# A decoder block in fp32 halves: narrower pooling columns, a second seven-product group in w_o, and another order at the front of the MLP

## The chip, the cores and the metric

One core of a Trainium2 chip. The time is device microseconds of one execution of the whole program; the figure for a kernel is the median of its timed runs. Beside the timed runs one execution is recorded by the hardware profiler, and the views below come from that one.

## The reference

One layer: a combined projection of the normed input, causal pooling over four windows, a gated depthwise convolution, two sigmoid gates, the projection w_o, and an MLP with squared relu. Sequence 256 behind 16 meta tokens, model width 2048, MLP width 8192, all fp32.

```python
u = rms_norm(h, g_pre_mix)                     # h: 16 meta rows and 256 tokens
z_pool, v_conv, g_conv, gate_a, gate_b = split(u @ w_in)
# pooling group g (256 columns of z): mean over the last 2, 4, 8 or 16 tokens, minus the token
y_a = causal_multiscale_pool(z_pool, w_pool_grp, pool_scale) @ w_pool_out
y_b = conformer_conv(v_conv, g_conv, w_dw, b_dw, ln_g, ln_b) @ w_conv_out
m = sigmoid(gate_a) * y_a + sigmoid(gate_b) * y_b
h = h + rms_norm(m @ w_o, g_post_mix)
u = rms_norm(h, g_pre_mlp)
f = square(relu(u @ w_up)) @ w_down
h = h + rms_norm(f, g_post_mlp)
return h[:, 16:]
```

## The kernel before

**Products in halves.** An fp32 weight block of 128 x 2048 elements (1 MB, tile `raw`) is loaded by a DMA on SP's queue, cast on ACT to a rounded `hi` (1.91 us), and subtracted on DVE to the rest `lo` (2.29 us). The activations exist as such a pair too. A product of the two is three terms, hi times both halves and lo times the high half; where 256 tokens stand in both halves of one 512-column operand, that is 8 matmuls with hi and 4 with lo for a 512-deep block, 12 with 512 columns.

**Stages, in the order of the trace.** Start and transposes of x (to 35 us), the projections for v and g (to 107), the projection for z (`project(..., mm=mm3, width=L)`, four calls, one for each pooling group, 96 matmuls of L = 272 columns each; to 154.6), the gates (to 329) with the pooling and the depthwise convolution on DVE beside them, the grouped pooling map `acc_grp`, the two output projections po and co (to 424.9), w_o (to 510.6), the residual and the transposes for the second norm (to about 547), and the MLP in pieces (to 1189).

**z and the pooling.** `evac_z` multiplies a PSUM tile of z by the row factor `rb` on DVE. `pool_items` sums windows by doubling: level g adds the previous level to itself, shifted by 2^g columns. A window of 2, 4, 8 or 16 tokens needs 2, 4, 8 or 16 columns at most ahead of the 256 tokens; all four groups have 16.

**w_o.** The weight is 4 x 4 blocks of 512 x 512, block (kb, n) being rows kb and columns n. STEPS lists the work in PE's order. `Xnk` (column block n, rows k) is a plain step: two products, one for each half of the tokens, into the banks c0n and c1n. P1 to P7 are the seven products of a fast 2 x 2 scheme on rows 0 and 1 and columns 0 and 1: each takes a sum of blocks of w_o (`add_rooms` on DVE, 2.29 us, or `add_second`, a DMA on POOL's queue that accumulates a block onto one that is there) and a sum of parts of m (`forms_o`, four of them), and goes to bank a, b or a c bank. `GIVES_O` says to which c banks a product is given further: ACT copies the bank to a part of `og`, DVE adds or subtracts it. Banks a and b take the place of the tiles `mt` in which the last part of m was transposed (PE at line 898, ACT's cast m<-mt at 902, DVE's subtraction m<-mt at 905). There are 31 products: seven P and two for each of twelve X. The residual's input h1 (2 MB) is loaded on POOL's queue ahead of the co projection (L944). The w_o blocks go through three to five rooms `raw`.

**The order.** The class `Plan` collects work items: an engine, a cost in us, what they read and write, and a lateness. PE and SP keep the order in which items were added. For the other engines due times are worked out backwards from PE's, and a simulation with the costs picks what starts next; `emit` then writes the instructions. So a cost or a lateness changes no instruction but can change the order on ACT, DVE and POOL. One plan covers w_o, another the MLP.

**The front of the MLP.** Up to L1831 the plan holds the end of the first up product (banks `acc_up`), eight squares of h1 on ACT (`square_h1`, L987 in the trace) for the second norm, their sum (`mean2`, L1540), the root, `diag2` (rsqrt at L446 to L450, the power of two p2 and its diagonal at L1550 to L1553, and five small operations for eps2 at L1554 to L1559), and the first MLP loads. `up_done` empties a bank: ACT copies half of it (half<-..., L1578), DVE adds the other half to it (F_raw<-half,..., L1585). The second up product goes into two banks `bank_u` (L496 with hi, L502 with lo). The splits of the blocks raw_a, raw_c and raw_m are casts at L1496 and subtractions at L1500.

Of the kernel before, what the change touches and what calls it, by code (L numbers as in the profile page):

```python
# [115 lines left out]
def hybrid_block(ctx: ExitStack, tc: tile.TileContext, ins: dict, out: bass.AP):  # L116
# [559 lines left out]

    def evac_z(j0):
        def f(j, acc):
            nc.vector.tensor_mul(z[:, j0 + j, :], acc[:, :L], rb)
# [12 lines left out]
    def pool_items(g):  # L692
# [7 lines left out]
        def add(q):  # L700
            def f():
                nc.vector.tensor_add(dst[:, q:q + GK, lo_:], src[:, q:q + GK, lo_:],
                                     src[:, q:q + GK, lo_ - w:L - w])
            return f
# [181 lines left out]

    pairs_room = big.tile([P, 3, 2 * T], F32, tag="ux", name="pairs")
# [55 lines left out]
    h1 = big.tile([P, NT, D], F32, tag="k8", bufs=2, name="h1")  # L943
    nc.gpsimd.dma_start(h1, xv)  # L944
# [52 lines left out]
    def m_of(k):  # L997
# [7 lines left out]
    B_OF = {"P1": (0, 0), "P2": (1, 0), "P3": (1, 1), "P5": (0, 0), "P6": (0, 0), "P4": (0, 0),  # L1005
            "P7": (1, 1)}
    A_OF = {"P1": (0, 0), "P2": (0, 1), "P4": (1, 1)}
    FORM_OF = {"P3": SA4, "P5": SA1, "P6": SA2, "P7": SA3}
    INTO = {"P1": "a", "P2": "c00", "P3": "c01", "P5": "b", "P6": "a", "P4": "c10", "P7": "a"}
# [13 lines left out]
    room_at = {(1, 0): 0, (2, 0): 1}  # L1023
    steps = STEPS.split()

    def raw_key(s):

        return B_OF[s] if s[0] == "P" else (int(s[2]), int(s[1]))

    def source_o(key):  # L1030
        return columns(w_o, key[0] * CK, CK, key[1] * CW)[0][0]
# [5 lines left out]
    for i, s in enumerate(steps):  # L1037
        key = raw_key(s)
        last_use[key] = i
        if s == "P4":  # L1040
            last_use[B_OF["P2"]] = i
        if key not in wanted and key not in room_at:
            wanted.append(key)
# [20 lines left out]
    def add_second(room):  # L1064

        src = source_o((0, 1))
# [10 lines left out]
    def split_room(i, room, rows=CK, up=False):  # L1077
# [13 lines left out]
        plan.add("ACT", 1.91, high, reads=(f"raw{room}",), writes=(f"hi{q}",))  # L1091
        plan.add("DVE", 2.29, low, reads=(f"raw{room}", f"hi{q}"), writes=(f"lo{q}",))

    def add_rooms(to, room):
        a_, b_ = room_of[to][:, :CK * CW], room_of[room][:, :CK * CW]
        plan.add("DVE", 2.29, lambda: nc.vector.tensor_add(a_, a_, b_),
                 reads=(f"raw{to}", f"raw{room}"), writes=(f"raw{to}",))

    def weights_o(i):
        s = steps[i]  # L1100
        room = room_at[raw_key(s)]
        if s == "P6":
            add_rooms(room, room_at[B_OF["P3"]])
            add_second(room_at[B_OF["P3"]])
        if s == "P4":
            add_rooms(room, room_at[B_OF["P2"]])
        if i >= 2:
            split_room(i, room)
        if s == "P1":
            add_second(room)  # L1110
        for key, last in last_use.items():
            if last == i:
                free_rooms.append(room_at[key])
        loads_o()

    def forms_o(f):
        dst, src, name = Sf[:, f[0], f[1]], A[:, f[0], f[1]], f"S{f[0]}{f[1]}"
        plan.add("ACT", 0.68, lambda: nc.scalar.copy(dst[:, :, 0, :], src), reads=("A",),
                 writes=(name,))
        plan.add("DVE", 0.70, lambda: nc.vector.tensor_sub(dst[:, :, 1, :], src,  # L1120
# [13 lines left out]
    begun = set()  # L1134

    def product_o(i):
# [15 lines left out]
        bank = INTO[s]  # L1152
        if s in A_OF:
            form, names = m_block(*A_OF[s]), []
        else:
            at_ = FORM_OF[s]
            form, names = (lambda k, a_: Sf[:, at_[0], at_[1], k, a_, :]), [f"S{at_[0]}{at_[1]}"]
        add(bank, form, names, s in ("P1", "P5") or bank not in begun, True)
        if s in GIVES_O:
            j = "ab".index(bank)  # L1160
            st = og[:, j, block(NB - 1)]
            plan.add("ACT", 0.62, lambda: nc.scalar.copy(st, banks_o[bank]), reads=(bank,),
                     writes=(f"st{j}",))
            for t, n, sign in GIVES_O[s]:
                def f(name=f"c{t}{n}", add_=(nc.vector.tensor_add if sign > 0 else
                                             nc.vector.tensor_sub)):
                    add_(banks_o[name], banks_o[name], st)
                plan.add("DVE", 0.69, f, reads=(f"st{j}",), writes=(f"c{t}{n}",))

    def new_banks(make, *names):  # L1170
        for name in names:
            def f(name=name):
                banks_o[name] = make(f"o_{name}")
            plan.add("PE", 0.0, f, writes=(name,) + (("mt0", "mt1") if name in "ab" else ()))

    def m_last(t):
# [3 lines left out]
        plan.add("ACT", 0.62, f_hi, reads=(f"mt{t}",), writes=(f"m3{t}",))  # L1180
        plan.add("DVE", 0.69, f_lo, reads=(f"mt{t}", f"m3{t}"), writes=(f"m3{t}",))
# [5 lines left out]
    def evac_o(n, t, bank):  # L1187
        plan.add("ACT", 0.92, lambda: square_of(banks_o[bank], norm1.ssq, t, n), reads=(bank,),
                 writes=("junk", f"ssq{t}"))
        plan.add("DVE", 0.69, lambda: last_factor(og[:, t, block(n)], banks_o[bank], n),  # L1190
                 reads=(bank, "g_mix"), writes=(f"og{t}{n}",))

    new_banks(acc_tile, "c00", "c10", "c01", "c11", "c02", "c12")
# [4 lines left out]
    for i in range(2):  # L1198
        weights_o(i)
    for i, s in enumerate(steps):  # L1200
# [5 lines left out]
        if s == "X30":  # L1206
# [3 lines left out]
        product_o(i)  # L1210
        if i == 0:
            for t in range(NT):
                m_last(t)
        done = {"P7": (0,), "X23": (2,), "X13": (1,)}.get(s, ())
        for n in done:
# [783 lines left out]
```

## Time and profile before

| what | value |
|---|---|
| timed runs, median (lowest to highest of 3) | 1194.74 us (1194.17 to 1195.89) |
| profiled execution | 1199.05 us, span 1197.3 us |
| mean granted clock of TensorE | 0.996 |
| HBM traffic over the span | 224 GB/s |
| idle time of PE that ended with a wait, all places | 8.5 us |

How to read it: the page gives busy time and its share of the span for each engine; PE is TensorE's matmuls, PEld its weight loads, DVE, ACT, POOL and SP the other engines and the queue that issues loads. A timeline row is a start, a length (both us), engine, line, operation, out<-in, and in brackets the idle time before it and what ended it. A window's row is its length, then busy time and instruction count of PE, PEld, DVE, ACT and POOL as far as they did anything, the granted clock, the DMA engines' share and GB/s.

### The profile page before, as it was taken

What the parts mean: (1) busy time and instruction counts of PE and PEld (TensorE: products, weight loads), DVE (VectorE), ACT (ScalarE), POOL (GpSimd) and SP (SyncE); (2) the same over time, 40 slices, a digit from 0 to 9 for tenths busy, and PEclk for the clock granted to TensorE, in tenths of its full rate; (3) what the DMA queues carried; (4) which work ended last, traced back from release to release, by engine and by line L of the source; (5) the groups of instructions that cost most, each with busy time, mean ns of one, the idle gap of its engine ahead of it and who ended that gap; (6) DMA issues with size and microseconds to landing.
All of it is one profiled execution on the core that took longest, in us unless ns stands there. A gap on an engine that the chain in (4) does not pass through costs nothing.

```text
span 1197.3 us, 15759 instructions
## 1 busy us (share of the span) xinstructions
PE 1180.4 (99%) x6363; PEld 1023.7 (85%) x6363; DVE 1020.5 (85%) x1097; ACT 680.9 (57%) x705; POOL 41.8 (3%) x48
## 2 busy tenths in 40 slices
PE   9999999999999999999999999999999999999997
PEld 9999988888888888897888888888888888887886
DVE  6899978999776778677988989899999889898965
ACT  6533344444583455565666657666666676676742
POOL 1000000000000000000000000000000000000000
PEclk9999999999999999999999999999999999999999
DMA  9655555656548578548779889898998988998971
GB/s 291 212 177 179 185 197 179 207 179 205 182 165 282 172 251 264 198 135 290 211 210 260 242 243 273 248 262 230 274 249 253 259 265 243 250 262 232 271 255 71
DMA packets 176811, 269.76 MB, mean 225 GB/s; under 512 B 4610, under 2 KB 92866, under 8 KB 175841
## 3 DMA queue, kind: packets, MB, share of 16 engines
q1 hardware_dynamic: 160432, 234.83, 59.1%
q0 software_dynamic: 15408, 32.66, 14.9%
q10 hardware_dynamic: 896, 1.25, 0.3%
q8 instruction: 50, 0.82, 0.3%
q14 instruction: 25, 0.20, 0.0%
HBM read 264.53 MB, written 4.19 MB: 224 GB/s over the span
## 4 chain that ended last, share of the span: by engine, by line
PE 87%; DMA 6%; DVE 2%; ACT 2%; issue 2%; DVEq 0%; POOLq 0%; ACTq 0%; SPq 0%
PE acc_gate L789 15%; PE bank_u L496 14%; PE bank_a L1715 9%; PE bank_u L502 7%; PE acc_up L1715 7%; PE o_c L1128 6%; DMA raw_m<-in_w_down_dram 6%; PE bank_b L1715 5%; PE acc_z L491 4%; PE acc_co L789 4%; PE acc_po L789 4%; PE acc_v L491 3%; PE acc_g L491 3%; PE acc_vg L491 2%; PE bank_u L1715 1%
## 5 line engine op out<-in xcount | busy, mean ns | idle before, releaser
L496 PE MATMUL bank_u<-m,hi 128*128 128x512 f32 x960 | 331.1, 391 | 2.6 <-DVE F_raw L1585 2.6
L502 PE MATMUL bank_u<-m,lo 128*128 128x256 f32 x960 | 265.9, 277 | 0.0
L276 ACT CAST hi<-raw 128x2048 fp32r<-128x2048 f32 (+2 forms) x94 | 151.0, 1619 | 191.5 <-PE acc_gate L789 64.0
L1500 DVE TENSOR_TENSOR lo<-raw_m,hi 128x2048 fp32r<-128x2048 f32 x85 | 194.4, 2287 | 34.2 <-ACT hi L1496 34.2
L496 PEld LDWEIGHTS bank_u<-m,hi 128*128 128x128 f32 x960 | 180.9, 188 | 41.1 <-DVE F_raw L1585 3.0
L279 DVE TENSOR_TENSOR lo<-raw,hi 128x2048 fp32r<-128x2048 f32 (+2 forms) x94 | 180.1, 1924 | 37.1 <-ACT hi L276 36.4
L1496 ACT CAST hi<-raw_m 128x2048 fp32r<-128x2048 f32 x85 | 161.8, 1911 | 75.1 <-PE bank_a L1715 23.0
L502 PEld LDWEIGHTS bank_u<-m,lo 128*128 128x128 f32 x960 | 180.9, 188 | 1.6
L789 PE MATMUL acc_gate<-hi,u_um 128*128 128x512 f32 x416 | 131.1, 389 | 0.0
L557 DVE SCALAR_TENSOR_TENSOR c<-a,taps,c 128x256 f32<-128x256 f32 x240 | 115.6, 483 | 6.8
L789 PEld LDWEIGHTS acc_gate<-hi,u_um 128*128 128x128 f32 x416 | 78.1, 188 | 16.1
L789 PE MATMUL acc_gate<-lo,u_um 128*128 128x512 f32 x208 | 80.9, 389 | 0.0
L1715 PE MATMUL bank_a<-hi,forms 128*128 128x512 f32 (+1 forms) x232 | 75.7, 388 | 4.1 <-DVE F_raw L1744 4.1
L1715 PE MATMUL bank_b<-hi,forms 128*128 128x512 f32 (+1 forms) x208 | 67.4, 386 | 0.0
L1128 PE MATMUL o_c<-hi,m 128*128 128x512 f32 x208 | 65.6, 390 | 0.0
L1578 ACT COPY half<-bank_u 128x256 f32<-128x256 f32 x60 | 22.3, 372 | 73.6 <-PE bank_u L502 73.6
L1715 PE MATMUL bank_a<-fourth_pair,forms 128*128 128x512 f32 (+1 forms) x252 | 59.9, 386 | 0.7 <-ACT st_Q L1753 0.7
L1500 DVE TENSOR_TENSOR lo<-raw_a,hi 128x2048 fp32r<-128x2048 f32 x21 | 48.0, 2286 | 12.4 <-ACT hi L1496 12.4
L1715 PEld LDWEIGHTS bank_a<-hi,forms 128*128 128x128 f32 x232 | 43.4, 188 | 15.1 <-issue 5.2
L1500 DVE TENSOR_TENSOR lo<-raw_c,hi 128x2048 fp32r<-128x2048 f32 x20 | 45.7, 2287 | 10.9 <-ACT hi L1496 10.9
L1715 PEld LDWEIGHTS bank_a<-fourth_pair,forms 128*128 128x128 f32 x252 | 45.2, 188 | 10.1 <-ACT st_Q L1753 1.1
L1496 ACT CAST hi<-raw_a 128x2048 fp32r<-128x2048 f32 x21 | 40.1, 1910 | 20.6 <-PE bank_u L496 10.8
(398 smaller groups left out, 2267.2 us busy)
## 6 DMA issues: line engine op xcount, KB each, us to landing
raw<-in_w_in_dram SPq DMA_DIRECT2D x52, 1024.0 KB, 5.1
raw_m<-in_w_up_dram SPq DMA_DIRECT2D x42, 1024.0 KB, 7.2
raw_m<-in_w_down_dram SPq DMA_DIRECT2D x35, 1024.0 KB, 5.3
raw_a<-in_w_down_dram SPq DMA_DIRECT2D x15, 1024.0 KB, 5.7
raw_c<-in_w_down_dram SPq DMA_DIRECT2D x14, 1024.0 KB, 5.8
raw_m<-in_w_down_dram POOLq DMA_DIRECT2D x12, 1024.0 KB, 10.8
raw_o<-in_w_o_dram SPq DMA_DIRECT2D x10, 1024.0 KB, 7.2
raw_a<-in_w_up_dram SPq DMA_DIRECT2D x9, 1024.0 KB, 7.5
```

Of the source, the lines that this page charges most:

```text
L276: nc.scalar.copy(hi[:, sl, cs], raw[:, sl, cs])
L279: nc.vector.tensor_sub(lo[:, sl, cs], raw[:, sl, cs], f32(hi[:, sl, cs]))
L491: nc.tensor.matmul(acc, w[:, k[0], cs], act[:, k[1], a, off:], start=first and n == 0, stop=last and n == 2)
L496: nc.tensor.matmul(acc.rearrange("p (a t) -> p a t", a=2)[:, :, ts], hi[:, k[0], cs], act[:, k[1], :, off + ts.start:off + ts.stop], start ...
L502: nc.tensor.matmul(acc[:, :T], lo[:, k[0], cs], act[:, k[1], 0, off:], start=False, stop=stop, skip_group_check=True)
L557: nc.vector.scalar_tensor_tensor(c, conv["a"][:, q, i:i + T], taps[:, q, i:i + 1], c, op0=ALU.mult, op1=ALU.add)
L789: nc.tensor.matmul(acc, act(kk)[:, a_, ts_], w_[:, k, :], start=kk == 0 and n == 0, stop=kk == nk - 1 and n == 2)
L1128: nc.tensor.matmul(acc, form(k, a_), box[w_][:, k, :], start=start and k == 0 and n == 0, stop=stop and k == CK - 1 and n == 2, skip_group ...
L1496: nc.scalar.copy(box["hi"], raw)
L1500: nc.vector.tensor_sub(box["lo"], raw, f32(box["hi"]))
L1578: nc.scalar.copy(box[j], accs[j][:, :T])
L1715: nc.tensor.matmul(acc, forms[h][:, f, k, a_, :], box[w_][:, k, cs], start=start and k == 0 and n == 0, stop=stop and k == KH - 1 and n == ...
```

## The change

Four edits. (1) The z projection computes for group g only the last 256 + 2^(g+1) columns, so 258, 260, 264 and 272, and the evacuation and the pooling adds write only those. (2) In w_o a second seven-product group R on rows 0 and 1 and columns 2 and 3 stands beside P: 14 products in the two groups and eight X steps, 30 products. P's two sums that need no other product (blocks (0,0)+(0,1) and (0,1)+(1,1)) are made ahead by four DMAs on POOL's queue (two copy, two accumulate) into a tile `early_sums`, which go out when the po projection has ended, as the load of h1 did; h1 is loaded on SP's queue at the step H of the list, behind the load of X32's block. P5 goes straight into the bank c11 and is given to c01. (3) A number of costs in both plans are changed. (4) The five operations for eps2 are an item of their own, later in the plan; the first two loads of the MLP plan cost nothing there.

```diff
+    def first_col(g):
+        return M - (2 << g)
...
-    for h in range(PW // HALF_CW):
-        project(u, KD, evac_z(h * HALF_CW // P), f"z{h}", mm=mm3, width=L, fill=2.5)
+    for h in range(NG):
+        project(u, KD, evac_z(h * HALF_CW // P), f"z{h}", mm=mm3, width=L - first_col(h),
+                fill=2.5)
...
+    early_sums = big.tile([P, 2, CK * CW], F32, tag="k8", bufs=2, name="early_sums")
+    for keys, op in ((((0, 0), (0, 1)), {}), (((0, 1), (1, 1)), {"accum_op": ALU.add})):
+        for e, key in enumerate(keys):
+            nc.gpsimd.dma_start(early_sums[:, e].rearrange("p (k c) -> p k c", k=CK),
+                                source_o(key), **op)
...
-    h1 = big.tile([P, NT, D], F32, tag="k8", bufs=2, name="h1")
-    nc.gpsimd.dma_start(h1, xv)
...
-    GIVES_O = {"P1": [(0, 0, 1)], "P6": [(0, 1, -1)], "P7": [(1, 0, 1), (1, 1, -1)],
-               "P5": [(0, 1, 1), (1, 1, 1)]}
-    STEPS = "P2 X02 X20 P1 X12 P3 X21 P5 X22 P6 X03 P4 X23 P7 X13 X30 X31 X32 X33"
+    COLS_OF = {"P": 0, "R": 2}
+    INTO = {"4": (1, 0), "2": (0, 0), "3": (0, 1), "5": (1, 1)}
+    GIVES_O = {"1": [(0, 0, 1)], "6": [(0, 1, -1)], "7": [(1, 0, 1), (1, 1, -1)],
+               "5": [(0, 1, 1)]}
+    STEPS = "P2 X02 P1 P5 P3 P6 X03 R1 P7 X22 P4 X12 R3 R5 X13 R6 H R2 R7 X23 R4 X32 X33"
...
+        if g == "R" and n in ("3", "6") and {g + "3", g + "6"} <= set(steps[:i + 1]):
+            add_second(g, room_at[block_key(g, "3")])
...
+        if i == load_h1:
+            plan.add("SP", 6.4, place_h1, writes=("raw5", "raw6"), late=2.0)
...
-        plan.add("SP", 3.1, lambda: nc.sync.dma_start(
+        ahead = len(room_at) <= 2
+        plan.add("SP", 0.0 if ahead else 3.1, lambda: nc.sync.dma_start(
             room_of[room].rearrange("p (k c) -> p k c", k=rows), src),
-            writes=(f"raw{room}",), late=3.6)
+            writes=(f"raw{room}",), late=len(room_at) if ahead else 3.6)
...
-            plan.add("ACT", 0.65, square_h1(t, n), reads=("h1",), writes=("junk", "ssq2"))
+            plan.add("ACT", 0.75, square_h1(t, n), reads=("h1",), writes=("junk", "ssq2"))
...
-    plan.add("DVE", 1.2, diag2, reads=("q2", "v2"), writes=("diag2",))
+    plan.add("DVE", 1.7, diag2, reads=("q2", "v2"), writes=("diag2",))
...
+        if (s, i) == ("U1b1", 1):
+            plan.add("DVE", 0.9, eps_of_scaled, reads=("diag2",), writes=("eps2",))
```

The strings that order the MLP's pieces are the same; from the third split of the MLP on, SP, POOL and DVE have the same order. Three places where instructions stand otherwise:

DVE at the head of w_o, before, from a form of m to the next splits (hi_75 and lo_75 are the third block's halves, the first step that isn't split ahead; A holds parts of m, mt the transposed last part):

```order
L1120 TENSOR_TENSOR forms_o_3711<-A_3382,forms_o_3711 128x4x128
L1089 TENSOR_TENSOR lo_75_3742<-raw_o2_3709,hi_75_3733 128x2048
L905 TENSOR_TENSOR m_3381<-mt_3_0_3737,m_3381 128x4x128
L905 TENSOR_TENSOR m_3381<-mt_3_1_3744,m_3381 128x4x128
L1120 TENSOR_TENSOR forms_o_3711<-A_3382,forms_o_3711 128x4x128 x2
L1089 TENSOR_TENSOR lo_76_3785<-raw_o_3710,hi_76_3766 128x2048
L1120 TENSOR_TENSOR forms_o_3711<-A_3382,forms_o_3711 128x4x128
```

The same place of the change, where lo_76 is the second split, of a tile of the early sums, and raw_o is added onto the other one for P6:

```order
L1160 TENSOR_TENSOR forms_o_3714<-A_3387,forms_o_3714 128x4x128
L1121 TENSOR_TENSOR lo_75_3740<-raw_o2_3712,hi_75_3736 128x2048
L1121 TENSOR_TENSOR lo_76_3768<-early_sums_3380,hi_76_3747 128x2048
L925 TENSOR_TENSOR m_3386<-mt_3_0_3742,m_3386 128x4x128
L925 TENSOR_TENSOR m_3386<-mt_3_1_3749,m_3386 128x4x128
L1132 TENSOR_TENSOR early_sums_3380<-early_sums_3380,raw_o_3713 128x2048
L1160 TENSOR_TENSOR forms_o_3714<-A_3387,forms_o_3714 128x4x128
```

The second split and the add stand where one split stood, with one on either side of m<-mt; on PE, P1 (`o_a`) follows one X step and no longer two.

DVE ahead of R7, in the change alone (lo_88 is R6's block, lo_89 R2's, lo_90 R7's; raw_74 += raw_o is the add for R6, and raw_74 += raw_73 the one for R4; behind the first of them POOL issues the DMA that accumulates (0,3) onto raw_o):

```order
L1121 TENSOR_TENSOR lo_86_4003<-raw_74_3669,hi_86_3998 128x2048
L1132 TENSOR_TENSOR raw_74_3669<-raw_74_3669,raw_o_3713 128x2048
L1121 TENSOR_TENSOR lo_87_4035<-raw_o2_3712,hi_87_4032 128x2048
L1121 TENSOR_TENSOR lo_88_4051<-raw_74_3669,hi_88_4049 128x2048
L1132 TENSOR_TENSOR raw_74_3669<-raw_74_3669,raw_73_3625 128x2048
L1121 TENSOR_TENSOR lo_89_4084<-raw_73_3625,hi_89_4065 128x2048
L1212 TENSOR_TENSOR o_c03_4018<-o_c03_4018,og_3703 128x512
L1008 TENSOR_TENSOR og_3703<-o_c01_3717,g_mix_3929 128x512
L1008 TENSOR_TENSOR og_3703<-o_c11_3718,g_mix_3929 128x512
L1121 TENSOR_TENSOR lo_90_4119<-raw_o_3713,hi_90_4103 128x2048
L1121 TENSOR_TENSOR lo_91_4124<-raw_o_3713,hi_91_4121 128x2048
```

And ACT beside it, where the copy og<-o_b empties the bank of R6 for R7:

```order
L1116 CAST hi_87_4032<-raw_o2_3712 128x2048
L1116 CAST hi_88_4049<-raw_74_3669 128x2048
L1116 CAST hi_89_4065<-raw_73_3625 128x2048
L1207 COPY og_3703<-o_c13_4019 128x512
L1005 ACTIVATE acking_offset=None)_1_0_4082,ssq_mix_3704<-o_c01_3717 128x512
L1005 ACTIVATE acking_offset=None)_1_1_4100,ssq_mix_3704<-o_c11_3718 128x512
L1116 CAST hi_90_4103<-raw_o_3713 128x2048
L1116 CAST hi_91_4121<-raw_o_3713 128x2048
L1207 COPY og_3703<-o_b_3790 128x512
```

Before, there is no such group at this place; P7's operand was made by an accumulating DMA too. R7's cast and split are hi_90 and lo_90, and the copy for R6 stands behind two casts.

DVE at the front of the MLP, before, from the last bank of the first up product to the split of raw_m (acc_up and bank_u are the banks of the first two up products, tot2 the second norm's sum, lo_0 and lo_1 the rests of raw_a and raw_c):

```order
L1540 TENSOR_REDUCE tot2_4632<-ssq2_4548 128x2
L1541 TENSOR_SCALAR tot2_4632<-tot2_4632 128x2
L1585 TENSOR_TENSOR F_raw_4538<-half_011_0_4630,acc_up00_3_4297 128x256
L1500 TENSOR_TENSOR lo_0_4657<-raw_a_4539,hi_0_4637 128x2048
L446 RECIPROCAL r2_4549<-rs_q_2_4655 128x2
L447 TENSOR_TENSOR rs_q_2_4655<-r2_4549 128x2
```

...and, behind the four other operations of rsqrt and those for p2, diag2 and eps2:

```order
L1559 TENSOR_SCALAR eps2_4551<-eps2_4551 128x2
L1500 TENSOR_TENSOR lo_1_4693<-raw_c_4540,hi_1_4676 128x2048
L1585 TENSOR_TENSOR F_raw_4538<-half_100_0_4711,bank_u0_4544 128x256
L1585 TENSOR_TENSOR F_raw_4538<-half_101_0_4731,bank_u1_4545 128x256
L1500 TENSOR_TENSOR lo_2_4736<-raw_m0_4541,hi_2_4733 128x2048
```

And now:

```order
L1558 TENSOR_TENSOR lo_0_4649<-raw_a_4553,hi_0_4644 128x2048
L1645 TENSOR_TENSOR F_raw_4552<-half_011_0_4647,acc_up00_3_4311 128x256
L1598 TENSOR_REDUCE tot2_4671<-ssq2_4562 128x2
L1599 TENSOR_SCALAR tot2_4671<-tot2_4671 128x2
L1558 TENSOR_TENSOR lo_1_4694<-raw_c_4554,hi_1_4690 128x2048
L1645 TENSOR_TENSOR F_raw_4552<-half_100_0_4712,bank_u0_4558 128x256
L446 RECIPROCAL r2_4563<-rs_q_2_4692 128x2
```

...and, behind the four other operations of rsqrt:

```order
L1608 TENSOR_SCALAR p2_4564<-r2_4563 128x2
L1611 TENSOR_SCALAR diag2_4721<-ident_88,p2_4564 128x128 x2
L1645 TENSOR_TENSOR F_raw_4552<-half_101_0_4741,bank_u1_4559 128x256
L1614 TENSOR_SCALAR eps2_4565<-r2_4563 128x2
L1617 TENSOR_TENSOR eps2_4565<-eps2_4565 128x2 x2
L1618 RECIPROCAL eps2_4565<-eps2_4565 128x2
L1619 TENSOR_SCALAR eps2_4565<-eps2_4565 128x2
L1558 TENSOR_TENSOR lo_2_4751<-raw_m0_4555,hi_2_4743 128x2048
```

The split of raw_a now stands ahead of the last acc_up bank, the split of raw_c and the first bank_u ahead of the norm; the second bank_u stands between the diagonal and the five operations for eps2. On ACT the cast of raw_a stands ahead of the last square of h1.

More of the change, by code (lines that the diff above doesn't have):

```diff
@@ L1210, in hybrid_block @@
         product_o(i)
+        for entry in list(gives):
+            if entry[1] in begun:
+                gives.remove(entry)
+                entry[2]()
         if i == 0:
```

153 lines of the change are left out of this document (93 added, 60 removed).

## The prediction

> **What bounds the kernel now.** I read the page first: the shares of the engines and the chain that ended last. Then the list of PE's waits, PE's busy time by windows, and the timelines of PE, DVE and ACT around the one long wait.
>
> ```profile
> span 1197.3 us, 15759 instructions
> PE 1180.4 (99%) x6363; PEld 1023.7 (85%) x6363; DVE 1020.5 (85%) x1097; ACT 680.9 (57%) x705; POOL 41.8 (3%) x48
> ...
> PE 87%; DMA 6%; DVE 2%; ACT 2%; issue 2%; DVEq 0%; POOLq 0%; ACTq 0%; SPq 0%
> ```
>
> PE is busy for 99% of the span, so time goes only where PE gets less work or where one of its few waits goes; DVE is the second engine with 85%. PE's waits are these:
>
> ```profile
> PE bank_a L1715 <- DVE F_raw L1744: 4.1, 3, 1.7
> PE bank_u L496 <- DVE F_raw L1585: 2.6, 1, 2.6
> PE idle L392 <- DVE rb L308: 1.1, 1, 1.1
> PE bank_a L1715 <- ACT st_Q L1753: 0.7, 1, 0.7
> ```
>
> They add up to 8.5 us. The 4.1 and 0.7 lie inside the MLP's pieces, whose order is not changed, and the 1.1 at the start: no term for them. The 2.6 stands at the second up product, where the change does move things. The profiled execution took 1199.05 us (span 1197.3 and 1.75 around it); the median of the timed runs, 1194.74, is 4.31 us lower. I form the sum as a difference within the profiled execution and take it off the median.
>
> **The z projection.** It keeps 384 matmuls but 96 each now have 258, 260, 264 and 272 columns. The windows of the z stage and of the grouped pooling map (256 columns):
>
> ```profile
> 107.28:154.64 47.36, 47.36 (x384) 47.14 (x383) 3.05 (x7) 1.00 0.55 178
> 329.27:335.04 5.77, 5.77 (x48) 5.56 (x47) 1.54 (x4) 2.67 (x7) 1.00 0.61 190
> ```
>
> The first gives 47.36/384 = 123.3 ns for 272 columns, the second 5.77/48 = 120.2 ns for 256: 0.19 ns a column. 96 x (14 + 12 + 8) = 3264 columns go, so 0.6 us by this slope. A 512-column matmul in w_o takes 2.72/12 = 227 ns (rows below), 0.44 ns a column, and by that 1.4 us would go. I take **-0.9**, nearer to the pair of rows that are of this kind, with -1.4 and -0.6 as ends while the start of a slice costs nothing; that it may cost something is the last rival. The Trainium skill, "TensorE: Matmul & The Clock Gate", section "Wait — 56ns, not 53.3ns?", gives a warm matmul N/2.4 GHz plus about 2.5 ns, 115.8 ns for 272 columns; the trace has 123.3, so its rule doesn't hold here as it stands, and its slope would make the term an estimated -1.4. The trimmed pooling adds and evacuations are DVE work under PE's gate products: nothing, as PE waits for DVE nowhere there.
>
> **One product less in w_o.** The chain of waits in this stage is PE alone (start, length, what):
>
> ```profile
> 424.87 2.72 PE o_c L1128 x12
> 427.60 0.87 PE mt L898 x8
> 428.47 10.92 PE o_c L1128 x48
> ```
>
> A product is 12 matmuls and 2.72 us. The stage had 31 (the seven P steps, and two in each of twelve X steps): 31 x 2.72 + 0.87 = 85.2 us of about 85.7, so nothing waits there. The change leaves 30 (14 in the groups P and R, and eight X steps). **-2.7**, if PE stays fed. That is the question, since the window of the stage reads (with a row of DVE's bank adds)
>
> ```profile
> 424.80:510.60 85.80, 85.80 (x387) 71.10 (x386) 64.18 (x55) 48.79 (x49) 3.18 (x3) 1.00 0.76 245
> ...
> 464.47 1.29 DVE L1167 TENSOR_TENSOR o_c<-o_c,og 128x512 f32<-128x512 f32 x2
> ```
>
> DVE is busy for 64.2 of 85.8 us. The change gives it three more splits and two more adds of blocks (2.29 us each, as below) and four more bank adds at 0.65: 5 x 2.29 + 4 x 0.65 = 14.1, so 78.3 us in some 85: 92%. ACT gets three casts of 1.91 and some copies, about 57 us: still far off. Two places come out late by the new order.
>
> **New wait at P1.** P1 writes a bank that held the last transposes, and DVE's subtraction m<-mt frees it. Of before, DVE and ACT:
>
> ```profile
> 429.35 2.29 DVE L1089 TENSOR_TENSOR lo<-raw_o,hi 128x2048 fp32r<-128x2048 f32 x1 [1.12 <-ACT hi L1084]
> 431.56 1.28 DVE L905 TENSOR_TENSOR m<-mt,m 128x512 fp32r<-128x512 f32 x2
> ...
> 427.41 1.91 ACT L1084 CAST hi<-raw_o 128x2048 fp32r<-128x2048 f32 x1
> 429.22 0.61 ACT L1118 CAST forms_o<-A 128x512 fp32r<-128x512 f32 x1
> 429.74 1.07 ACT L902 CAST m<-mt 128x512 fp32r<-128x512 f32 x2
> ```
>
> m<-mt began at 431.56, and two X steps (four products) stood ahead of P1 on PE. Now one X step does: P1 is wanted at 428.47 + 2 x 2.72 = 433.9. DVE has a second split (of early_sums) ahead of m<-mt, so m<-mt runs from about 433.85 to 435.1. **+1.2**; +0.6 if the first half is enough. ACT casts m<-mt behind one more cast too, at 431.6 to 432.7, early enough. Behind m<-mt DVE has only the add for P6, two steps away.
>
> **New wait at R7.** R7's operand is a block on which POOL accumulates another one by DMA, issued behind DVE's add for R6. From 429.35 the new order has 12 splits, 3 adds of blocks, and 13 operations of 0.65 on DVE up to and with that add: 15 x 2.29 + 13 x 0.65 = 42.8, so the DMA goes out at about 472.2. Then come ACT's cast (1.91) and DVE's split (2.29): ready at 476.4 plus the landing time. PE wants it at 424.87 + 0.87 + 22 x 2.72 + 1.2 = 486.8, the split 0.2 later. So the wait is the landing time less 10.6. Such DMAs in this stage (median us last), and over the MLP (min, median, max):
>
> ```profile
> raw_o<-in_w_o_dram POOLq DMA_DIRECT2D x1, 1024.0 KB, 10.5
> g_mix<-in_g_post_mix_dram POOLq DMA_DIRECT2D x1, 1024.0 KB, 12.9
> raw<-in_w_o_dram POOLq DMA_DIRECT2D x1, 1024.0 KB, 9.9
> ...
> DMA to landing us min/median/max: 8.8/10.0/15.9
> ```
>
> The residual's 2 MB load moves to SP and can run just beside it, so I take 12, between 9.9 and 15.9 and nearer to the rows of this stage: **+1.4**, with ends 0 and 5.3.
>
> **Early sums and the residual's load.** Four POOL DMAs of 1 MB stand where one of 2 MB stood, beside the loads for the co products. The 16 engines are busy there to
>
> ```profile
> 378.60:405.00 26.40, 26.40 (x122) 21.90 (x122) 15.51 (x14) 11.71 (x9) 0.75 (x1) 1.00 0.68 240
> 405.00:424.80 19.80, 19.80 (x97) 16.54 (x96) 18.14 (x19) 8.86 (x9) 0.00 (x0) 1.00 0.46 158
> ```
>
> 68% and 46%, which leaves 8.4 + 10.7 = 19.1 us. POOL's queue, and the first use of the residual:
>
> ```profile
> q0 software_dynamic: 15408, 32.66, 14.9%
> ...
> 520.60 0.74 DVE L993 SCALAR_TENSOR_TENSOR h<-og,r_mix,h 128x512 f32<-128x512 f32 x1
> ```
>
> 14.9% of the span for 32.66 MB is 5.5 us a MB; two MB more are 11 us. That fits into both windows, not into the first alone. I take 0, as the sums are first wanted at about 430, and +2 as the end if the co loads come late. The residual's load goes out right behind that of X32's block, which PE wants cast and split by 499; it is wanted itself at 520.60, over 20 us later: 0.
>
> **The wait ahead of the second up product.** PE's row, the windows on both sides of it, then DVE and ACT:
>
> ```profile
> 550.25 0.79 PE L496 MATMUL bank_u<-m,hi 128*128 128x512 f32 x1 [2.65 <-DVE F_raw L1585]
> ...
> 547.30:550.20 2.90, 0.30 (x2) 0.00 (x0) 2.87 (x5) 2.17 (x2) 0.00 (x0) 0.98 0.96 377
> 550.20:553.60 3.40, 3.35 (x11) 2.87 (x12) 2.52 (x2) 0.00 (x0) 0.00 (x0) 0.52 1.03 351
> ...
> 542.88 2.29 DVE L1500 TENSOR_TENSOR lo<-raw_a,hi 128x2048 fp32r<-128x2048 f32 x1 [1.38 <-ACT hi L1496]
> 545.08 0.16 DVE L446 RECIPROCAL r<-rs_q 128x2 f32<-128x2 f32 x1
> 547.57 2.29 DVE L1500 TENSOR_TENSOR lo<-raw_c,hi 128x2048 fp32r<-128x2048 f32 x1
> 549.78 0.74 DVE L1585 TENSOR_TENSOR F_raw<-half,bank_u 128x256 f32<-128x256 f32 x2
> ...
> 540.94 1.91 ACT L1496 CAST hi<-raw_a 128x2048 fp32r<-128x2048 f32 x1
> 542.84 1.90 ACT L1496 CAST hi<-raw_c 128x2048 fp32r<-128x2048 f32 x1
> ```
>
> The banks were full at 547.3, but DVE came to empty them at 549.78, behind the norm's small operations (545.08 to 547.57) and the split of raw_c. It costs twice: 2.7 us of idle, and then a clock of 0.52 for 3.4 us, 1.6 us more. The Trainium skill, same page, section "HAM oscillation — how this bites in real kernels", warns of gaps over about 3.4 us; here 2.65 us lowered the clock, so the row decides; by the page only the 2.7 would be there to gain. In the new order the last of the eight squares stands behind the cast of raw_a, which so starts 0.9 us earlier, at 540.1; DVE splits raw_a from 542.0 to 544.3, empties the last acc_up bank and sums the squares until 544.9 (0.6 us), splits raw_c, and F_raw<-half,bank_u comes right behind at 547.2, before the norm. So the first bank is free at 547.6, just when PE ends its last matmul ahead of it (550.25 - 2.65); I allow 0.3 us for what I may have missed. The second bank follows the norm (1.6 us) at 549.6, when PE is still filling the first. **-4.0** of 4.3: 2.4 of idle and all of the slow clock, as the 1.67 us wait (the longest of the 4.1 above) is followed by a clock of 1.00:
>
> ```profile
> 1089.00:1092.50 3.50, 3.26 (x15) 2.73 (x16) 3.50 (x3) 3.47 (x3) 0.00 (x0) 1.00 0.60 202
> ```
>
> What is late next is a transfer: the DMA share of 0.96 to 1.03 says that raw tiles come at the limit there. The five small operations for eps stay ahead of the split of raw_m, but behind both banks: nothing for PE.
>
> **Sum.** -0.9 - 2.7 + 1.2 + 1.4 - 4.0 = -5.0: 1199.05 would become 1194.05, and 1194.74 becomes **1189.7**. Anything under 0.2%, 2.4 us, is about what a measurement of this kernel cannot tell from no change.
>
> **The rivals.**
> - *The front's wait stays, under another name.* For it: the DMA share above, and that all loads there share 16 engines that are full; PE arrives 4 us earlier at loads that are no faster. Against: before, ACT cast raw_m when PE freed buffers, not on landing. Then -4.0 becomes about 0: 1193.7. Chance 0.17.
> - *The accumulated operand of R7 lands at the worst row's 15.9.* +5.3 for +1.4: 1193.6. For it: the 2 MB beside it; against: 9.9 and 10.5 in this stage. Chance 0.12. DVE at 92% is the same case with the add later.
> - *Both new waits are hidden* (landing at 10, half of m<-mt enough): +0.6 for +2.6: 1187.7. Chance 0.13.
> - *Slower: slices that start inside a row of u are read slower.* The moving operand of 288 matmuls now starts 14, 12 or 8 columns in; no matmul of the trace does. At nothing per matmul the forecast stands; from (5.0 + 2.4)/288, 26 ns each (a fifth of 123.3), the kernel is over 2.4 us slower. At half the speed, which the rows show for the slow clock (0.52), it is 288 x 123 ns = +35: 1225; at 30 ns each 1198.3. Nothing in the trace speaks for it, and nothing excludes it. Chance 0.08.
> - The forecast holds with the rest, 0.50.
>
> **How the numbers follow.** Faster by over 0.2% (below 1192.35): the forecast, the hidden waits, and a third of the two cases near 1193.7, which may come in part: 0.50 + 0.13 + 0.10 = 0.73. Within 0.2%: the rest of those, 0.19. Slower: 0.08. The range goes from 1187.0 (the hidden waits, z at -1.4) to 1194.6 (a middle rival with z at nothing); beyond lie the slower case and both middle rivals at once.
>
> **What would show it.** The z window at about 46.4 us with 384 matmuls (over 47.4: the offset costs). In w_o 12 matmuls fewer, a wait of PE at P1 near 434 for DVE m, one at R7 near 487 for DVE lo with ACT behind a DMA. At the second up product no wait over 0.5 us and a clock of 1.0. Wrong if a new row on the list of PE's waits exceeds 2 us, or if PE waits in the MLP where it did not.

## The result, and the profile after

The changed kernel takes 1191.09 us (median of 12 runs, 1189.4 to 1192.62), the kernel before 1194.45 us in the 12 runs beside them (1192.45 to 1197.66). The ratio is 0.9966, with a 95% interval of 0.9957 to 0.9975: 4.1 us less, between 3.0 and 5.1, by the ratio. (The medians are 3.4 apart.) A second measurement of the same two kernels, e9 below, gave 3.2 us less, between 2.2 and 4.4. The forecast was 5.0 less. Runs in an undisturbed state alone are compared. The sign and the order of size were right; the make-up of the sum was not, as follows.

The page of the changed kernel, and the list of PE's waits:

```profile
span 1188.1 us, 15764 instructions
PE 1174.9 (99%) x6351; PEld 1018.3 (86%) x6351; DVE 1033.6 (87%) x1106; ACT 688.8 (58%) x712; POOL 44.9 (4%) x51
```

```profile
PE bank_a L1775 <- DVE F_raw L1804: 2.3, 3, 1.0
PE idle L392 <- DVE rb L308: 1.1, 1, 1.1
PE o_a L1168 <- DVE m L925: 0.7, 1, 0.7
PE bank_a L1775 <- ACT st_Q L1813: 0.7, 1, 0.7
```

12 matmuls are gone (6363 to 6351), the wait for DVE F_raw at bank_u is gone, P1's wait (o_a) is new, and R7's isn't there. The span is 9.2 us shorter than the one profiled before, much more than the timed runs are apart. A comparison of these two traces alone would have credited the change with twice what it does; that is what the first experiment is about.

**z.** The window of the z projection:

```profile
106.46:152.64 46.18, 46.18 (x384) 45.96 (x383) 2.97 (x7) 1.00 0.56 184
```

46.18 us where 47.36 stood: -1.18, or 0.36 ns for each of the 3264 columns.

**w_o.** The window of the stage, then the chain through it:

```profile
422.60:508.00 85.40, 84.67 (x383) 69.60 (x383) 78.24 (x70) 57.08 (x58) 3.10 (x3) 1.00 0.78 256
```

```profile
422.80 2.74 PE o_c L1168 x12
...
431.85 0.69 DVE m L925
432.55 0.04 issue
432.59 3.02 PE o_a L1168 x12
...
484.70 2.77 PE o_b L1168 x12
```

And PE's rows around P1, from the last matmul ahead of it to the first behind it:

```profile
431.47 0.39 PE L1168 MATMUL o_c<-hi,m 128*128 128x512 f32 x1
432.59 0.50 PE L1168 MATMUL o_a<-hi,m 128*128 128x512 f32 x1 [0.73 <-DVE m L925]
432.93 0.40 PE L1168 MATMUL o_a<-lo,m 128*128 128x512 f32 x1
...
435.44 0.39 PE L1168 MATMUL o_c<-hi,forms_o 128*128 128x512 f32 x1
```

DVE is busy for 78.24 us, the prediction's 78.3, and PE stands idle at P1 for 0.73 us, until the first half of m<-mt is done (431.85 + 0.69). A matmul starts 0.23 us behind the one ahead of it where nothing waits, so P1 was due at 431.70 and came 0.89 late; its own second matmul starts 0.34 behind the first, and the next product 2.85 us behind P1 and not 2.72. That is 1.0 us in all where 1.2 was forecast. R7's product takes 2.77 us: no wait. From its first matmul to that of the first up product the stage takes 84.6 us; it took 86.1.

Why R7 didn't wait, by the rows of POOL, ACT and DVE, and of the landing of POOL's DMA and of the residual's:

```profile
470.14 1.27 POOL L1099 DMA_DIRECT2D raw_o<-in_w_o_dram  x1 [21.47 <-DVE raw L1132]
...
479.94 1.90 ACT L1116 CAST hi<-raw_o 128x2048 fp32r<-128x2048 f32 x1
...
481.87 4.49 DVE L1121 TENSOR_TENSOR lo<-raw_o,hi 128x2048 fp32r<-128x2048 f32 x2
```

```profile
h<-in_x_dram SPq DMA_DIRECT2D x1, 2048.0 KB, 12.9
...
raw_o<-in_w_o_dram POOLq DMA_DIRECT2D x1, 1024.0 KB, 9.0
```

The DMA went out 2 us earlier on the trace's clock than the sum had put it, as the whole stage did, and landed after 9.0 us, not 12; in the six other profiles with this w_o and this DMA (e3, e5, e7 to e10) it landed after 9.1 to 9.4. By the prediction's rule (landing time less 10.6) that leaves 1.6 us in hand; e11 will put it at 1.2. The residual's load beside it took 12.9 us, and nobody waited for it.

**The front of the MLP.** ACT, DVE, and the windows where PE had stood still:

```profile
535.56 1.90 ACT L1554 CAST hi<-raw_a 128x2048 fp32r<-128x2048 f32 x1
...
537.49 2.29 DVE L1558 TENSOR_TENSOR lo<-raw_a,hi 128x2048 fp32r<-128x2048 f32 x1 [1.94 <-ACT hi L1554]
540.63 2.29 DVE L1558 TENSOR_TENSOR lo<-raw_c,hi 128x2048 fp32r<-128x2048 f32 x1 [0.24 <-ACT hi L1554]
542.84 0.42 DVE L1645 TENSOR_TENSOR F_raw<-half,bank_u 128x256 f32<-128x256 f32 x1
544.87 0.42 DVE L1645 TENSOR_TENSOR F_raw<-half,bank_u 128x256 f32<-128x256 f32 x1
```

```profile
543.30:546.50 3.20, 3.20 (x20) 2.79 (x19) 2.49 (x14) 2.04 (x2) 0.00 (x0) 1.00 0.97 380
546.50:550.00 3.50, 3.50 (x22) 3.04 (x21) 2.29 (x1) 0.14 (x1) 0.00 (x0) 1.00 1.04 359
```

The first bank of the second up product is emptied right behind the split of raw_c, the second behind the norm, as the forecast had it. PE runs through, at a clock of 1.00, with the DMA share still at 0.97 to 1.04.

### The profile page after: what moved, and what is told of

It reads as the page before. It is cut to its first block, busy times and chain, and to the rows that moved or that the text cites. A ratio compares the mean times of both kernels' runs of the same rounds, so it can differ in the third digit from the quotient of the medians.

```text
span 1188.1 us, 15764 instructions
## 1 busy us (share of the span) xinstructions
PE 1174.9 (99%) x6351; PEld 1018.3 (86%) x6351; DVE 1033.6 (87%) x1106; ACT 688.8 (58%) x712; POOL 44.9 (4%) x51
## 4 chain that ended last, share of the span: by engine, by line
PE 89%; DMA 6%; ACT 2%; DVE 2%; issue 2%; DVEq 0%; POOLq 0%; ACTq 0%
PE bank_u L496 15%; PE acc_gate L800 15%; PE bank_a L1775 9%; PE bank_u L502 7%; PE acc_up L1775 7%; DMA raw_m<-in_w_down_dram 6%; PE bank_b L1775 6%; PE o_c L1168 5%; PE acc_z L491 4%; PE acc_co L800 4%; PE acc_po L800 4%; PE acc_v L491 3%; PE acc_g L491 3%; PE acc_vg L491 2%; PE acc_up L496 1%
## 5 line engine op out<-in xcount | busy, mean ns | idle before, releaser
L1775 PEld LDWEIGHTS bank_a<-hi,forms 128*128 128x128 f32 x232 | 43.4, 188 | 13.6 <-issue 3.9
L1168 PE MATMUL o_c<-hi,m 128*128 128x512 f32 x160 | 50.9, 391 | 0.0
L1554 ACT CAST hi<-raw_a 128x2048 fp32r<-128x2048 f32 x21 | 40.1, 1909 | 18.5 <-PE bank_u L496 10.8
```

The costliest lines, as they stand in the source:

```text
L1168: nc.tensor.matmul(acc, form(k, a_), box[w_][:, k, :], start=start and k == 0 and n == 0, stop=stop and k == CK - 1 and n == 2, skip_group ...
L1554: nc.scalar.copy(box["hi"], raw)
L1775: nc.tensor.matmul(acc, forms[h][:, f, k, a_, :], box[w_][:, k, cs], start=start and k == 0 and n == 0, stop=stop and k == KH - 1 and n == ...
```

## The experiments

All ran beside runs of the kernel before on the same chip: one chip for e1 to e4, one for e5 to e8, one for e9 to e11 and one for e12.

| run | what it is | median us | ratio to before (95%) |
|---|---|---|---|
| e1 | before, again | 1195.25 | 1.0002 (0.9986 to 1.0019) |
| e2 | z alone | 1194.11 | 0.9990 (0.9976 to 1.0004) |
| e3 | w_o alone | 1194.44 | 0.9995 (0.9982 to 1.0008) |
| e4 | the front's plan alone | 1193.63 | 0.9984 (0.9973 to 0.9995) |
| e5 | z and w_o, front as before | 1192.18 | 0.9979 (0.9969 to 0.9988) |
| e6 | before, DVE delayed at the front | 1197.62 | 1.0023 (1.0014 to 1.0031) |
| e7 | the change, P5 ahead of P1 | 1190.14 | 0.9960 (0.9948 to 0.9972) |
| e8 | the change, z from the first column | 1190.7 (one run) | |
| e9 | the change, again | 1191.66 | 0.9973 (0.9963 to 0.9982) |
| e10 | e7's kernel, again | 1190.23 | 0.9957 (0.9943 to 0.9971) |
| e11 | the change, R7's operand late | 1202.49 | 1.0064 (1.0048 to 1.0079) |
| e12 | before, one load late | 1199.75 | 1.0035 (1.0017 to 1.0053) |

From the traces, worked out as the time from the first matmul of one group to the first of the next (us): the z stage, w_o to the first up product, and from the start of the second up product to that of the kernel's last matmul.

| kernel | z | w_o | second up product to the last matmul |
|---|---|---|---|
| before, first profile | 47.4 | 86.1 | 652.1 |
| e1, before again | 47.4 | 86.1 | 649.6 |
| e2, z alone | 46.2 | 86.1 | 648.6 |
| e3, w_o alone | 47.4 | 84.5 | 649.2 |
| e4, front alone | 47.4 | 86.1 | 649.8 |
| e5, z and w_o | 46.2 | 84.6 | 648.4 |
| after, first profile | 46.2 | 84.6 | 646.5 |
| e9, after again | 46.2 | 84.5 | 649.1 |
| e7, P5 ahead of P1 | 46.2 | 83.6 | 645.8 |
| e10, the same again | 46.2 | 83.6 | 647.8 |

z and w_o repeat to 0.2 us. The last column differs by 2.5 and 2.6 us between two profiles of one kernel.

### e1: the kernel before, a second time

> The kernel of before, unchanged, for a second profile of it. Ratio 1.000 within its interval. Theory A (the stall ahead of the second up product, 2.65 us of idle and 1.6 us of half clock, stands in every execution): the profile shows a wait for DVE F_raw of 2 to 3 us near 550 and a window with a clock of about 0.5 behind it. Theory B (that one profiled execution, 4.6 us above the median, was unusually slow at this place): the wait is under 1.5 us or the clock behind it stays at 1.0, and the profiled span is about 1193 us.

The row and the windows of its front:

```profile
548.63 0.50 PE L496 MATMUL bank_u<-m,hi 128*128 128x512 f32 x1 [1.55 <-DVE F_raw L1585]
```

```profile
545.00:548.70 3.70, 2.15 (x13) 1.63 (x12) 3.56 (x9) 1.58 (x2) 0.00 (x0) 1.00 1.02 407
548.70:552.20 3.50, 3.50 (x20) 3.04 (x21) 2.50 (x2) 0.59 (x1) 0.00 (x0) 1.00 0.99 345
```

The wait is 1.55 us and the clock behind it 1.00; the profiled execution took 1195.8 us. Theory B holds to this extent: the wait is there in both executions, but with 1.1 us less idle and without the slow clock.

### e2 to e4: each part alone

> Before with the narrower z columns alone. By the z window of the changed kernel (46.18 us for 384 matmuls against 47.36) 1.2 us less, so -0.10%, whatever the rest does; a rival, that the start of a slice inside a row costs something, would give no gain and a z window of 47 us or more.

```diff
-        project(u, KD, evac_z(h * HALF_CW // P), f"z{h}", mm=mm3, width=L, fill=2.5)
+        project(u, KD, evac_z(h * HALF_CW // P), f"z{h}", mm=mm3, width=L - first_col(h),
+                fill=2.5)
```

Its z stage took 46.2 us as in the whole change; the ratio of 0.9990 is the expected size, though its interval takes in 1. Its wait ahead of the second up product was 1.48 us.

> Before with the two seven-product groups, the early sums and the w_o costs alone; the z projection and the MLP's front plan as before. The prediction's terms (-2.7 + 1.2 + 1.4) give -0.1 us; the changed kernel's trace (one wait of 0.73 at P1, none at R7) gives -2.0 us or -0.17%. PE's waits should list P1 at 0.7 and no R7. Theory A keeps a wait of 2 to 3 us ahead of the second up product.

```diff
-    STEPS = "P2 X02 X20 P1 X12 P3 X21 P5 X22 P6 X03 P4 X23 P7 X13 X30 X31 X32 X33"
+    STEPS = "P2 X02 P1 P5 P3 P6 X03 R1 P7 X22 P4 X12 R3 R5 X13 R6 H R2 R7 X23 R4 X32 X33"
```

The stage is 1.6 us shorter; the time can't be told from no change (0.9995), nor from the expected 2.0 us less, which lies just inside the interval. The wait ahead of the second up product was 2.22 us in its profile, and the clock stayed at 1.00 behind it:

```profile
548.15 0.50 PE L496 MATMUL bank_u<-m,hi 128*128 128x512 f32 x1 [2.22 <-DVE F_raw L1631]
```

```profile
548.20:551.70 3.50, 3.50 (x20) 3.04 (x21) 2.43 (x2) 0.00 (x0) 0.00 (x0) 1.00 1.01 334
```

So it looked as if that wait took back part of the gain: the question of e5.

> Before with the costs of the MLP's front alone (loads, squares, diag2, eps2 apart). Theory A: -4 us, -0.33%, no wait ahead of the second up product and a clock of 1.0. Theory B: at most -1.5 us, as the usual execution had less to lose there. Theory C (the wait goes but PE meets the transfers of the next blocks earlier and waits there instead): no gain, and new waits of PE behind a DMA or DVE within some 50 us of it.

```diff
-    plan.add("DVE", 1.2, diag2, reads=("q2", "v2"), writes=("diag2",))
+    plan.add("DVE", 1.7, diag2, reads=("q2", "v2"), writes=("diag2",))
...
+        if (s, i) == ("U1b1", 1):
+            plan.add("DVE", 0.9, eps_of_scaled, reads=("diag2",), writes=("eps2",))
```

(with the other costs of the MLP's plan). 0.9984 is 1.9 us, between 0.6 and 3.2: theory B's size, not theory A's 4. The wait is gone. Of the waits inside the MLP this execution had more than any other,

```profile
PE bank_a L1718 <- DVE F_raw L1747: 5.2, 5, 1.4
```

against 4.1 and 3.5 us in the two profiles of before, 2.3 and 3.1 in the two of after: they vary with the execution. The first of these five waits comes at 753.75 us, some 200 us behind the place, and the timed runs are faster: both speak against theory C.

### e5: is w_o's gain given back at the front?

> The changed kernel with the MLP's front plan of before: z and w_o edits only. Theory G (given back: the chain of DVE and ACT at the front hangs on the transfer that lands ahead of it and not on PE, so what PE gains in w_o it waits for there): the wait ahead of the second up product is longer than the 1.5 us of the second profile of before, 2.2 us or more, and the ratio to before is that of z with little of w_o, 0.9985 to 0.9995. Rival A (terms are independent): wait of 1.5 us, ratio 0.9978 (-1.2 and -1.4 us).

```profile
546.12 0.51 PE L496 MATMUL bank_u<-m,hi 128*128 128x512 f32 x1 [1.54 <-DVE F_raw L1642]
```

1.54 us, as in e1, although PE came 2.5 us earlier, and 0.9979 for the independent terms' 0.9978. Theory G, which e3 had suggested, falls. What is ahead of the wait moves with PE: the load that the wait hangs on (e12) goes out 14.9 us behind the first matmul of the first up product in before, e1, e3 and e5 alike. The 2.22 us of e3 come from how long that load took.

### e6: the price of the clock

```diff
         nc.vector.tensor_scalar(eps2, eps2, RMS_EPS, None, op0=ALU.mult)
+        for _ in range(7):
+            nc.vector.tensor_scalar(eps2, eps2, 1.0, None, op0=ALU.mult)
```

> Before with seven more small DVE operations (0.2 us each, times one) behind eps2 ahead of the split of raw_c, so 1.4 us more wait ahead of the second up product: 1.5 + 1.4 = 2.9 us. Theory T (a wait of somewhat over 2.2 us lowers the granted clock for the next 3.4 us): a window with a clock of about 0.5 behind it, and 1.4 + 1.6 = 3 us more than before, ratio 1.0025. Rival: the slow clock of the first profile had another cause; the clock stays at 1.0 and the ratio is 1.0012.

```profile
550.05 0.50 PE L496 MATMUL bank_u<-m,hi 128*128 128x512 f32 x1 [3.08 <-DVE F_raw L1587]
```

```profile
549.90:553.30 3.40, 3.25 (x13) 2.84 (x14) 2.63 (x3) 0.00 (x0) 0.00 (x0) 0.68 1.01 324
553.30:556.70 3.40, 3.40 (x18) 2.93 (x17) 0.00 (x0) 0.00 (x0) 0.00 (x0) 0.82 1.07 378
```

Theory T holds: the wait of 3.08 us is followed by 3.40 x 0.32 + 3.40 x 0.18 = 1.7 us lost to the clock, and the kernel is 0.23% slower (2.7 us, between 1.7 and 3.7) for 1.5 us more of wait. All waits of 2.65 us and more seen here did that. Below it the length alone doesn't decide: e3's 2.22 us left the clock at 1.00, and one of 1.99 us inside the MLP of e9 lowered it. Where the wait falls does. In all fourteen profiles the granted clock changes, behind its first rise, only at whole multiples of 3.413 us from that rise (at the 159th in before, the 160th in e6, the 243rd in e9). Cut by these slots, the rows of before, of e3 and of e9:

```profile
546.66:550.07 3.41, 0.94 (x6) 0.59 (x4) 3.27 (x8) 2.17 (x2) 0.00 (x0) 1.00 0.95 380
550.07:553.48 3.41, 3.23 (x10) 2.75 (x11) 2.65 (x3) 0.00 (x0) 0.00 (x0) 0.50 1.05 356
...
543.57:546.98 3.41, 2.37 (x14) 1.83 (x13) 3.16 (x11) 1.06 (x3) 0.00 (x0) 1.00 1.05 441
546.98:550.39 3.41, 2.23 (x13) 1.97 (x14) 3.41 (x4) 1.17 (x1) 0.00 (x0) 1.00 0.95 325
550.39:553.80 3.41, 3.41 (x22) 2.95 (x21) 0.24 (x1) 0.00 (x0) 0.00 (x0) 1.00 1.05 359
...
831.27:834.68 3.41, 1.42 (x7) 0.91 (x6) 3.41 (x4) 0.90 (x2) 0.00 (x0) 1.00 0.48 159
834.68:838.09 3.41, 3.41 (x9) 2.63 (x9) 3.41 (x2) 2.86 (x2) 0.00 (x0) 0.50 0.57 164
```

PE stood for 2.5 us of the slot in before (3.41 less 0.94) and for 2.0 of the one in e9, and the next slot has half the clock. A slot's edge cuts e3's wait into 1.0 and 1.2 us, and neither part lowers it. So it is in all fourteen: a slot at full clock in which PE stood for 1.99 us or more was followed by one at half, a slot with 1.67 us or less by one at full clock. The next slot is at full clock again if PE is busy in the low one; with 1.72 us or more of standing in it (e11, e12) it is low too.

### e12: what sets the length of the wait

```diff
+            if n == 80:
+                nc.sync.dma_start(raw[:, :2], src[:, :2])
             nc.sync.dma_start(raw, src)
```

> Before with a quarter of one load made twice: the last block of the first up product, whose transfer took 5.7, 6.1, 6.1, 6.5 and 6.9 us in five profiles in which the wait ahead of the second up product was 1.48, 1.55, 1.54, 2.22 and 2.65 us. Theory D (that transfer sets the wait, through ACT's cast, the squares behind it and DVE's splits): the block lands 2.5 to 5 us later than 6.1, the wait grows by nearly as much, to 4 to 6 us, with a half clock behind it: 4 to 7 us more than before, ratio 1.0035 to 1.006. Rival (transfer and wait only move together because both follow how busy the DMA engines are): the wait stays at 1.5 to 2.7 us.

The small load landed 2.6 us after its issue, and the whole block 6.1 us after its own: 8.7 us in all.

```profile
525.51 2.62 DMA raw<-in_w_up_dram
528.15 6.11 DMA raw<-in_w_up_dram
```

PE's wait, and the clock behind it:

```profile
PE bank_u L498 <- DVE F_raw L1587: 4.5, 1, 4.5
```

```profile
551.70:555.10 3.40, 3.10 (x9) 2.67 (x10) 2.78 (x3) 0.00 (x0) 0.00 (x0) 0.50 0.98 336
```

2.6 us later, 3.0 us more wait than e1: theory D holds. The ratio of 1.0035 is at the lower end of what was expected. The chain is that transfer, ACT's cast, the eight squares behind it, the casts of raw_a and raw_c, and DVE's splits. From the issue of the load to the start of ACT's cast it is 5.76 us in e2, 6.50 in e3, 6.93 in the first profile of before and 8.83 in e12; the waits, 1.48, 2.22, 2.65 and 4.55, are each 4.28 us less. In e1 and e5 it is 6.13 us, and the waits of 1.55 and 1.54 are another 0.3 less, as PE came to the place 37.09 us behind the start of the first up product and not 36.79. So the first profile of before was simply the execution with the longest transfer of the five, 6.9 us.

### e7, e10: P1's wait taken away

```diff
-    STEPS = "P2 X02 P1 P5 P3 P6 X03 R1 P7 X22 P4 X12 R3 R5 X13 R6 H R2 R7 X23 R4 X32 X33"
+    STEPS = "P2 X02 P5 P1 P3 P6 X03 R1 P7 X22 P4 X12 R3 R5 X13 R6 H R2 R7 X23 R4 X32 X33"
...
-        plan.add("DVE", 0.62, f_lo, reads=(f"mt{t}", f"m3{t}"), writes=(f"m3{t}",))
+        plan.add("DVE", 0.62, f_lo, reads=(f"mt{t}", f"m3{t}"), writes=(f"m3{t}",), late=1.0)
```

> The changed kernel with P5 ahead of P1 on PE and m<-mt ahead of the next add on DVE. If P1's wait of 0.73 us is the bank that m<-mt frees, no wait over 0.3 us is left at P1 and the w_o stage is 0.7 us shorter (84.0 by the start of the first up product against 84.7), ratio to before about 0.9960. Rival: P5's cast and split, of the early sums, become late in its place, with a wait of 0.5 us or more at o_c.

> P5 ahead of P1 again, for a comparison with the changed kernel on the same chip: 1.0 us less (the w_o stage was 83.6 us by the start of the first up product against 84.7), a ratio to before 0.0009 lower than the changed kernel's. Rival: the 1.0 us is lost again further on, and the two ratios are equal within 0.0003.

The chain through e7's stage (P2, X02 and P5, then P1):

```profile
422.97 2.72 PE o_c L1168 x12
425.69 0.87 PE mt L918 x8
426.56 8.21 PE o_c L1168 x36
434.77 2.72 PE o_a L1168 x12
```

No stop, P1 at 2.72 us, the stage 83.6 us both times, so 0.9 to 1.0 less where 0.7 was expected (the wait alone, without what the stop costs beside it). The two edits were not tried apart. Beside each other, 0.9957 to 0.9973 is 0.0016 less than the change, where 0.0009 was expected; the two intervals overlap, so the order of the two kernels is shown by the stage and only supported by the times. It is the fastest version measured here.

### e8: does a slice that starts inside a row cost anything?

```diff
-            nc.tensor.matmul(acc, w[:, k[0], cs], act[:, k[1], a, off:],
+            nc.tensor.matmul(acc, w[:, k[0], cs], act[:, k[1], a, :acc.shape[1]],
```

> The changed kernel with z's 258, 260, 264 and 272 columns taken from the first column of u and no longer from the last (so z is that of other tokens). If the start inside a row costs nothing, the z window stays at 46.2 us; if it costs, it is shorter, down to 45.9 by 0.44 ns for each of the 3264 columns left out of 47.36.

```profile
106.92 46.51 PE acc_z L496 x384
```

46.51 us from the first column, 46.18 from column 14, 12 and 8: a start inside the row costs nothing. This kernel takes z of other tokens, so it serves for the time alone. The expectation had it the same or shorter; it is 0.3 us longer, in one profile. The difference lies in the two narrowest groups (11.59 and 11.53 us for 11.43 and 11.39), and why stays open.

### e11: R7's transfer, late

```diff
+            if twice:
+                nc.gpsimd.dma_start(room_view(room), again)
             nc.gpsimd.dma_start(room_view(room), src, accum_op=ALU.add)
```

> The changed kernel with R7's operand loaded once more by POOL ahead of the accumulation, so that it lands twice as late, about 16 to 18 us after the issue and not 9.0. By the prediction's rule (wait at R7 is the landing time less 10.6) PE waits 5.4 to 7.4 us at R7, where the profile lists DVE lo, and the granted clock falls to about a half for the next 3.4 us as the wait is over 2.7 us: 7 to 9 us more than the changed kernel, ratio to before 1.002 to 1.005. Rival: the transfer has more slack than that, since X23 and R4 stand behind it and PE's queue isn't held; then less than 2 us.

```profile
494.15 0.80 PE L1174 MATMUL o_b<-hi,forms_o 128*128 128x512 f32 x1 [9.26 <-ACT og L1213]
```

```profile
489.92 3.70 ACT L1122 CAST hi<-raw_o 128x2048 fp32r<-128x2048 f32 x2 [9.68 <-DMA raw_o<-in_w_o_dram]
493.52 0.58 ACT L1213 COPY og<-o_b 128x512 f32<-128x512 f32 x1
```

The accumulation went out at 476.19 and landed 13.6 us later, 19.5 us after the first DMA's issue at 470.37: later than the 16 to 18 expected, so the cost came out above the expected 7 to 9 us as well. The rule gives 19.5 - 10.6 = 8.9 us; PE waited 9.26, in the end not for DVE's split, as the rule has it, but for the copy og<-o_b, which stands behind two casts on ACT. The landing less the wait is 10.2 us, so a landing after 9.0 us has 1.2 in hand and not 1.6. In the profile the stage is 11.9 us longer than in e9: the wait, and 2.6 for the 5.1 us that PE then ran at a clock of 0.50. By the timed runs it is 10.8 (1202.49 and 1191.66). The prediction's mechanism is real and its place right; its rule names the wrong last step and is 0.4 us off.

## Why the prediction was right, and where it wasn't

- **z: -0.9 forecast, -1.2 measured.** Within its ends of -0.6 and -1.4. 0.36 ns a column lies between the two slopes. The Trainium skill ("TensorE: Matmul & The Clock Gate", "Wait — 56ns, not 53.3ns?") has 1/2.4 ns a column, which would be an estimated -1.4; the trace, with 0.36 ns and -1.2, doesn't agree.
- **One product: -2.7.** 12 matmuls of 227 ns are gone; right.
- **P1: +1.2 forecast, 1.0 measured,** at the place and for the operation given, but not by its whole length: the first half of m<-mt was enough, for which the prediction had +0.6. m<-mt began 9.2 us into the stage where the sum has 9.0, so P1 came 0.9 late, and 0.1 goes at the restart.
- **R7: +1.4 forecast, 0 measured.** The step that failed is the landing time, "I take 12": it was 9.0, and 9.4 at most in seven profiles. The residual's load was taken to slow POOL's DMA; beside it the DMA landed sooner than the 9.9 and 10.5 us of the trace of before. So w_o gave -1.5 where -0.1 was forecast.
- **Early sums: 0 forecast, 0 measured.** From the first matmul of the gates to the first of w_o it is 270.2 us in the profiles of before and of the change.
- **The front: "-4.0 of 4.3" forecast, 1.5 us by e1 and e5's waits and 1.9 (0.6 to 3.2) by e4.** The mechanism was right in each step, and which operations stand where came out as worked out. The size was that of one execution. Its 2.65 us of idle and 1.6 us of slow clock were read from a profile whose time, 1199.05 us, stood 4.3 us above the median; the prediction said so and still took the whole difference off the median. In the four other profiles with the old order at this place and no delay added (e1, e2, e3, e5) the wait is 1.55, 1.48, 2.22 and 1.54 us and costs no clock; all five together have a mean of 1.9.
- **The sum.** -1.2 - 1.5 - 1.5 = -4.2, and -4.6 with 1.9 for the front; the ratio gave 4.1 (3.0 to 5.1), and e9 3.2 (2.2 to 4.4). The forecast's -5.0 was 2.1 to 2.5 too much at the front and 1.7 too little elsewhere (1.4 in w_o, 0.3 in z): it came near by luck, because two errors went opposite ways.
- **The rivals.** That a transfer takes the front's wait over: no such wait in either profile of after. The wait inside the MLP at 915 us of after (1.02 us), which the first profile of before lacks, stands in e1 too (at 920, 0.84 us), so it isn't the change's. R7's late transfer: didn't happen; by e11 a landing after 15.9 us would have cost 5.7 us of waiting where +5.3 was said, and the slow clock behind it, for which the rival had nothing. Slices that start inside a row: no cost (e8). Both waits hidden: R7's was, P1's not.

What stays open is why the transfer at the front takes 5.7 us in one execution and 6.9 in another, and why the waits inside the MLP come to 2.3 us in one and 5.2 in another. In e9 one of them had the slow clock behind it, 1.7 us, which is most of the 2.6 between the two profiles of after in the last column of the table.

## What to carry to other kernels

Before a stall in a profile is priced, ask how far that execution lies from the median: a stall that follows a transfer's landing differs from one execution to the next, and a second profile of the unchanged kernel would have shown 1.5 us for 4.3. Price a wait with what follows it: here a wait of 2.0 us or more costs 1.7 more in the clock if that much of it falls into one slot of 3.41 us, and nothing more if a slot's edge cuts it small enough; where the slots lie differs from one execution to the next. When a product or a step is taken out, list what the other engines had done under it: P1's bank had been free 6.6 us ahead of P1 (439.39 in the chain of before, less 432.84); two products less (5.4) and a split more (2.3) make that a wait of 1.1 by this sum, and 1.0 was measured.

## What the hardware showed that I had not expected

A wait of PE of 2.65 or 3.08 us brought 3.41 us of half clock and one of 4.55 us twice that; waits of 2.04 (e10) and 2.22 us brought none, but one of 1.99 us did: the length alone doesn't decide, the standing inside one slot of 3.41 us does. The half clock needn't stand in one window of mine: after 3.08 us it showed as 0.68 and 0.82 in two. The Trainium skill ("TensorE: Matmul & The Clock Gate", "HAM oscillation — how this bites in real kernels") puts the limit at about 3.4 us; the runs here put it between 1.67 and 1.99 us within a slot. The Trainium skill ("TensorE: Matmul & The Clock Gate", "What's actually happening") has the clock judged over a window of about 3.4 us that runs on by itself; the traces agree, with slots of 3.413 us whose first edge lies 4.3 to 7.4 us behind the first instruction, at another place in each execution. And a 1 MB DMA on POOL's queue that accumulates landed in 9.0 us beside a 2 MB load on SP's queue that took 12.9 us, while the load of the same 2 MB took 10.4 on POOL's queue before.
